# Layer 1's first norm on places that are free early and with its roots in PSUM; layer 1's second modulation range computed beside layer 0's latent attention; half of layer 0's last scatter in place

## The chip, the cores and the metric

The kernel runs on one NeuronCore of a Trainium2 chip. Its engines run side by side, each through its own instruction queue in order: TensorE (PE in the profile; PEld is its weight loading), VectorE (DVE), ScalarE (ACT), GpSimd (POOL) and SyncE (SP), whose queue issues nearly all DMAs. The metric is the device time of one execution in microseconds; three runs of the kernel before gave a median of 1532.29 us (1531.54 to 1534.32).

## The reference

A backbone of two layers over 256 latent and 256 context tokens of 1024 channels, in float32. Each layer is a mixer and then a mixture of experts (MoE); both are entered through an RMS norm with a scale and shift ("modulation") computed from a condition vector, and left through a gate.

```
ml = split(silu(c) @ ada_w[l] + ada_b[l], 6)      # six modulation vectors; mc likewise from c_ctx
n  = rmsnorm(h, norm1_g[l]) * (1 + ml[1]) + ml[0]
h  = h + ml[2] * mixer(n)                          # layer 0: conv + differential attention; layer 1: gated linear attention
n  = rmsnorm(h, norm2_g[l]) * (1 + ml[4]) + ml[3]
h  = h + ml[5] * hier_moe(n)                       # 32 experts, top group of 4, top 2 of 8 inside it
rmsnorm(x, g) = x / sqrt(mean(x^2) + eps) * g
```

Layer 0 computes all 512 tokens; layer 1 ends with the 256 latent ones. The output is the latent stream.

## The kernel before

The program is written straight through as mixer0, the MoE of layer 0, mixer1, the MoE of layer 1. The tile framework gives every engine its queue by its own estimate of times and by priorities (a stretch written under `later()` is put behind), so a line that is moved can change the order of others around it. `order` rows below show the queues that came out.

*Tokens.* `H` holds the residual stream, four blocks of 128 tokens (blocks 0 and 1 latent, 2 and 3 context). `XH` and `XL` hold the mixer's or MoE's transposed input, split into a rounded part and a rest, so that a product is three TensorE passes (`mm3`, L288 to L293).

*Weights.* `wtile()` hands out 1 MB places of a ring, four in the mixers and more in the MoEs. A load into a place waits until the place's earlier weights have been read. A weight is split by `quarter` (L366 to L373): ACT rounds it (`wh`, L371), POOL or DVE subtracts (`wl`, L372).

*Modulation.* `ada_steps(l, r, ...)` computes range r (0, 1 or 2, a third of the six vectors each) in eight steps. A step loads 1 MB of `ada_w` (L196) and does four matmuls of 32 x 512 (L201); the eighth adds the bias (L210). It is a generator: each `next()` is one step, so the steps can be laid among other work. `ada_cols` (L267, L270) transposes range 0 into columns that the norm uses.

*mixer0.* After the projections come four attention blocks (`attn_block`), two latent and two context. Each block's four heads call `fill(i)`; for the latent blocks `fill_lat` takes one step of `ada_steps(1, 0)`, for the context blocks `fill_ctx` takes two quarters of the latent rows' output projection (`out_lat`). The four loads of `ab_w_out` (`ts`, L359) use the same ring of four as the `ada` steps and stand behind them on SP.

*MoE of layer 0.* `scatter0` (L1491 to L1502) adds a pair of expert groups to `H`: for each of four blocks and two halves of the channels four matmuls into one of two `wk` PSUM banks (L1498), a multiplication by the gate into an SBUF tile `sc` (L1501, DVE), and an addition to `H` (L1502: POOL for half 0, DVE for half 1). The last call ends the MoE and feeds mixer1.

*mixer1.* `norm_mod_T` (L318 to L342), called for the latent and then the context stream, squares two blocks on ACT (L325) into tiles `xn` of the pool `raw1`, takes the reciprocal roots on DVE (`rstd_of`, L273 to L286: nine instructions on 128x2, all in SBUF), scales (L328 on DVE, L329 on ACT), transposes on PE (L335), modulates on DVE (L340), rounds on ACT to `XH` (L341) and subtracts to `XL` (L342: DVE for even k, POOL for odd). The small weights of the decay (`wf`, L820 to L827) are loaded by SP and split by ACT (L874, L879) and DVE (L875, L880). `ada_steps(1, 1)` runs here, its eight loads into four tiles that are free then (`S`, `sg`, `bT`, `attb`). The q projection follows (L870), then k, decay, levels, v, gate and output.

Of the kernel before, what the change touches and what calls it, by code (L numbers as in the profile page):

```python
# [9 lines left out]
FT = mybir.dt.float32  # L10
FR = mybir.dt.float32r
BF = mybir.dt.bfloat16
I32 = mybir.dt.int32
U32 = mybir.dt.uint32
AF = mybir.ActivationFunctionType
OP = mybir.AluOpType
# [3 lines left out]
D = 1024  # L20
# [10 lines left out]
EPS = 1e-6  # L31
# [49 lines left out]
def trunk_kernel(ctx: ExitStack, tc: tile.TileContext, A: dict, out: bass.AP):  # L81
    nc = tc.nc
# [9 lines left out]
    def pj(dt=FT):  # L92
        return psum.tile([128, 512], dt, name="pj", tag="pj", bufs=4)
# [6 lines left out]
    def wk(dt=FT):  # L100
        return wkp[0].tile([128, 512], dt, name="wk", tag="wk", bufs=2)
# [39 lines left out]
    H = const.tile([128, 4, D], FT, name="H")  # L141
# [112 lines left out]
    cols1 = [None]  # L254
# [18 lines left out]
    def rstd_of(dst, ss, n, pool, temps=None):  # L273
# [9 lines left out]
        for a in (2.38924456, 3 / c ** 2):  # L283
            nc.vector.tensor_mul(t, dst, dst)
            nc.vector.tensor_mul(t, t, w)
            nc.vector.scalar_tensor_tensor(dst, t, -a, dst, op0=OP.add, op1=OP.mult)  # L286

    def mm3(ps, st, mv, k0, k1):  # L288

        (sh, sl), (mh, ml) = st, mv  # L290
        nc.tensor.matmul(ps, sh, mh, start=k0, stop=False)  # L291
        nc.tensor.matmul(ps, sh, ml, start=False, stop=False)  # L292
        nc.tensor.matmul(ps, sl, mh, start=False, stop=k1)  # L293
# [21 lines left out]
                else:  # L315
                    nc.scalar.activation(o, v, AF.Copy)

    def norm_mod_T(pool, st, cols):  # L318

        ss = pool.tile([128, 2], FT, name="ss", tag="ss", bufs=2)  # L320
        rs = pool.tile([128, 2], FT, name="rs", tag="rs", bufs=2)
        xs = []
        for i in range(2):
            x = pool.tile([128, D], FT, name="xn", tag="xn", bufs=4)
            nc.scalar.activation(x, H[:, 2 * st + i], AF.Square, accum_out=ss[:, i:i + 1])  # L325
            xs.append(x)
        rstd_of(rs, ss, D, pool)
        nc.vector.tensor_scalar(xs[0], H[:, 2 * st], rs[:, 0:1], None, op0=OP.mult)  # L328
        nc.scalar.activation(xs[1], H[:, 2 * st + 1], AF.Copy, scale=rs[:, 1:2])  # L329
        t = slice(256 * st, 256 * st + 256)  # L330
        for kp in range(4):
            ps = trps()
            for j in range(4):
                k = 2 * kp + j // 2
                nc.tensor.transpose(ps[:, j * 128:(j + 1) * 128], xs[j % 2][:, k * 128:(k + 1) * 128], ident)  # L335
            for kk in range(2):
                k = 2 * kp + kk
                v = ps[:, kk * 256:kk * 256 + 256]
                a = pool.tile([128, 256], FT, name="xa", tag="xa", bufs=4)
                nc.vector.tensor_scalar(a, v, cols[:, 1, k, st:st + 1], cols[:, 0, k, st:st + 1], op0=OP.mult, op1=OP.add)  # L340
                nc.scalar.activation(XH[:, k, t], a, AF.Copy)  # L341
                (nc.gpsimd if kk else nc.vector).tensor_sub(XL[:, k, t], a, XH[:, k, t].bitcast(FT))  # L342
# [56 lines left out]
    def mixer0():  # L399
        es = ExitStack()  # L400
        with es:
# [3 lines left out]
            bp = pool(es2, "b0", "left")  # L405
# [310 lines left out]
                    k = 2 * q + kk  # L716
                    mm3(ps, (ch[:, k, t], cl[:, k, t]), (w[0][:, kk], w[1][:, kk]), k == 0, k == 7)

            ad = ada_steps(1, 0, bp)
            ts = []  # L720

            def fill_lat(i):
                next(ad, None)

            def out_lat():
                for n in range(2):
# [19 lines left out]
                attn_block(b, fill_lat)  # L746
            for _ in ad:
                pass
            cols1[0] = ada_cols(1)
            ts += [load_cols(w, [(512 * n, 512)]) for n in range(2)]  # L750
            es6.close()
            es2.close()
# [31 lines left out]
    def mixer1():  # L784
        es = ExitStack()
        with es:
# [44 lines left out]
            def split2(x0, x1):  # L831

                hl = [xp.tile([128, 1024], FR, name="w" + t, tag="ws" + t, bufs=3) for t in "hl"]
                for i, x in enumerate((x0, x1)):
# [8 lines left out]
            tsq = load_cols(w_in, [(0, 512)])  # L843


            free = [S.rearrange("p a h e -> p (a h e)"), sg.rearrange("p b c -> p (b c)"),
                    bT.rearrange("p a h t -> p (a h t)"), attb]

            fill = ada_steps(1, 1, mp, free[::-1])
            cols = cols1[0]  # L850
            for st in range(2):
                norm_mod_T(rp, st, cols)
            for _ in fill:
                pass
            es2.close()
            es4 = ExitStack()
            lp = pool(es4, "gl1", "right")
# [14 lines left out]


            nc.scalar.activation(wa2s[0], wa2, AF.Copy)  # L874
            nc.vector.tensor_sub(wa2s[1], wa2, wa2s[0].bitcast(FT))  # L875
            wah, wal = (ep.tile([128, 8, 128], FR, name="wv", tag="Ev", bufs=3) for _ in range(2))
            w4 = [waf.rearrange("p k (d j) -> p k d j", d=2)] + [w.rearrange("p k (d c j) -> p k d c j", d=2, c=2) for w in (wah, wal)]
            for c in range(2):
                nc.scalar.activation(w4[1][:, :, :, c], w4[0], AF.Copy)  # L879
                nc.vector.tensor_sub(w4[2][:, :, :, c], w4[0], w4[1][:, :, :, c].bitcast(FT))  # L880
            ps = wk()
            for k in range(8):
                mm3(ps, (wah[:, k], wal[:, k]), (xh[:, k], xl[:, k]), k == 0, k == 7)
# [352 lines left out]
    def moe(M):  # L1236
# [15 lines left out]
        with es:  # L1252
# [99 lines left out]
            with es2:  # L1352
# [135 lines left out]
                            if last:  # L1488
                                (nc.scalar if hf else nc.sync).dma_start(out[0, b * 128:(b + 1) * 128, c], H[:, b, c])

                def scatter0(Gs, ys):  # L1491

                    for b in range(nb):
                        for hf in range(2):
                            ps = wk()
                            n = 2 * len(Gs)
                            for i in range(n):
                                nc.tensor.matmul(ps, Gs[i // 2][:, b * 128:(b + 1) * 128], ys[i // 2][i % 2][:, hf], start=i == 0, stop=i == n - 1)  # L1498
                            c = slice(512 * hf, 512 * hf + 512)
                            t = ep.tile([128, 512], FT, name="sc", tag="sc", bufs=2)  # L1500
                            nc.vector.tensor_mul(t, ps, g2[:, b // 2, c])  # L1501
                            (nc.vector if hf else nc.gpsimd).tensor_add(H[:, b, c], H[:, b, c], t)  # L1502
# [233 lines left out]
                if l == 0:  # L1736
# [24 lines left out]
                    for j in range(0, NG, 2):  # L1761
# [29 lines left out]
                        prev = ([G[:, x] for x in range(2)], ys)  # L1791
                        if nxt:
                            (xgT, G), gc = nxt, gcn
                    scatter0(*prev)
                else:
                    P0 = group_hot(groups[0], pos0)
                    crowded()
# [57 lines left out]
```

## Time and profile before

| what | value |
|---|---|
| median of three runs | 1532.29 us |
| profiled execution | 1534.05 us, of which the trace's span 1532.3 us |
| PE busy | 1287.3 us (84% of the span) |
| DVE, ACT, POOL busy | 573.5, 367.9, 280.0 us |
| DMA | 498.10 MB, mean 325 GB/s |

The profile covers one execution. Its page gives the busy time of each engine, 40 slices of the span, the DMA queues, the chain of work that ended last, and the costliest groups of instructions. The trace behind it can be asked for the instructions of a stretch in order of time, or for the busy time of each engine in given stretches. The granted clock of TensorE (PEclk) is a share of full speed: 1.00 is 2.4 GHz and 0.50 is 1.2 GHz. The stages of the kernel by the trace: mixer0 to about 340 us, the MoE of layer 0 to about 835, mixer1 to about 1060, the MoE of layer 1 to the end.

### The profile page before, as it was taken

What the parts mean: (1) busy time and instruction counts of PE and PEld (TensorE: products, weight loads), DVE (VectorE), ACT (ScalarE), POOL (GpSimd) and SP (SyncE); (2) the same over time, 40 slices, a digit from 0 to 9 for tenths busy, and PEclk for the clock granted to TensorE, in tenths of its full rate; (3) what the DMA queues carried; (4) which work ended last, traced back from release to release, by engine and by line L of the source; (5) the groups of instructions that cost most, each with busy time, mean ns of one, the idle gap of its engine ahead of it and who ended that gap; (6) DMA issues with size and microseconds to landing.
All of it is one profiled execution on the core that took longest, in us unless ns stands there. A gap on an engine that the chain in (4) does not pass through costs nothing. (4 is left out here: it accounts for less than half of the span.)

```text
span 1532.3 us, 19009 instructions
## 1 busy us (share of the span) xinstructions
PE 1287.3 (84%) x7485; PEld 659.9 (43%) x7485; DVE 573.5 (37%) x1182; ACT 367.9 (24%) x700; POOL 280.0 (18%) x190
## 2 busy tenths in 40 slices
PE   5998978788789899999987999997966778777776
PEld 4665636564234344443422677775412222222221
DVE  4489895753002131221205546766202012112111
ACT  3245563441010101010102484434100000000000
POOL 1467601421001010100103543452000000000000
PEclk9999997798999999999998999999898889999889
DMA  9857361156999999999999634468799999999996
GB/s 318 286 203 248 118 220 51 64 203 280 421 422 424 422 422 422 376 423 422 423 423 390 221 101 138 166 224 323 299 426 427 426 427 427 427 427 427 427 427 281
DMA packets 101133, 498.10 MB, mean 325 GB/s; under 512 B 17654, under 2 KB 30297, under 8 KB 46253
## 3 DMA queue, kind: packets, MB, share of 16 engines
q1 hardware_dynamic: 96796, 489.84, 79.7%
q0 software_dynamic: 1680, 6.16, 1.3%
q8 instruction: 61, 1.00, 0.2%
q10 hardware_dynamic: 2560, 0.81, 0.2%
q14 instruction: 36, 0.29, 0.0%
HBM read 495.68 MB, written 1.10 MB: 324 GB/s over the span
## 5 line engine op out<-in xcount | busy, mean ns | idle before, releaser
L1561 PE MATMUL pj<-wx,xgT 128*32 128x512 f32 (+1 forms) x1496 | 312.8, 645 | 70.1 <-DMA wx<-in_moe_w_dram 70.1
L1561 PE MATMUL pj<-wt,xgT 128*32 128x512 f32 (+1 forms) x704 | 164.4, 639 | 26.4 <-DMA wt<-in_moe_w_dram 22.5
L1561 PEld LDWEIGHTS pj<-wx,xgT 128*32 128x32 f32 (+1 forms) x1496 | 75.7, 120 | 256.5 <-DMA wx<-in_moe_w_dram 130.6
L1570 PE MATMUL pj<-wx,hT 128*32 128x512 f32 (+1 forms) x792 | 166.7, 604 | 9.1 <-DMA wx<-in_moe_w_dram 5.1
L1453 DVE SCALAR_TENSOR_TENSOR s<-s,gc,pj 128x512 f32<-128x512 f32 x20 | 14.9, 747 | 421.6 <-PE pj L1561 368.3
L372 POOL TENSOR_TENSOR wl<-wt,wh 128x1024 fp32r<-128x1024 f32 x50 | 124.8, 2504 | 159.8 <-ACT wh L371 152.8
L291 PE MATMUL pj<-wh,XH 128*128 128x512 f32 x304 | 124.4, 419 | 17.2 <-ACT p L623 9.6
L292 PE MATMUL pj<-wl,XH 128*128 128x512 f32 x304 | 125.1, 411 | 1.6 <-POOL wl L372 1.5
L293 PE MATMUL pj<-wh,XL 128*128 128x512 f32 x304 | 123.7, 408 | 0.2
L1502 POOL TENSOR_TENSOR H<-H,sc 128x512 f32<-128x512 f32 x24 | 30.7, 1278 | 396.6 <-DVE sc L1501 396.6
L371 ACT ACTIVATE wh<-wt 128x1024 fp32r<-128x1024 f32 x66 | 68.9, 1055 | 66.7 <-PE pj L293 46.7
L1561 PEld LDWEIGHTS pj<-wt,xgT 128*32 128x32 f32 (+1 forms) x704 | 38.4, 120 | 104.9 <-issue 58.7
L1570 PEld LDWEIGHTS pj<-wx,hT 128*32 128x32 f32 (+1 forms) x792 | 42.6, 113 | 93.0 <-issue 70.5
L291 PEld LDWEIGHTS pj<-wh,XH 128*128 128x128 f32 x304 | 59.2, 196 | 46.7 <-ACT p L623 11.0
L1452 ACT ACTIVATE s<-pj 128x512 f32<-128x512 f32 x20 | 12.0, 598 | 252.7 <-PE pj L1561 252.7
L1458 ACT ACTIVATE hT<-trps 128x512 f32<-128x512 f32 x20 | 11.9, 597 | 247.3 <-PE trps L1456 247.3
L545 DVE SCALAR_TENSOR_TENSOR wk<-hp,vt,wk 128x512 f32<-128x512 f32 x90 | 67.5, 750 | 1.7
L292 PEld LDWEIGHTS pj<-wl,XH 128*128 128x128 f32 x304 | 59.7, 196 | 18.1 <-issue 3.2
L293 PEld LDWEIGHTS pj<-wh,XL 128*128 128x128 f32 x304 | 59.4, 195 | 14.5 <-DVE XL L1096 1.2
L1570 PE MATMUL pj<-wt,hT 128*32 128x512 f32 (+1 forms) x280 | 56.0, 611 | 2.8 <-ACT hT L1458 2.8
L1388 PE MATMUL wk<-P,XH 128*128 128x256 f32 x192 | 50.8, 300 | 5.2 <-ACT xgT L1390 3.8
L1501 DVE TENSOR_TENSOR sc<-wk,g 128x512 f32<-128x512 f32 x48 | 32.2, 687 | 44.2 <-PE wk L1498 44.2
(470 smaller groups left out, 1980.1 us busy)
## 6 DMA issues: line engine op xcount, KB each, us to landing
wx<-in_moe_w_dram SPq DMA_DIRECT2D x266, 1024.0 KB, 19.6
wt<-in_moe_w_dram SPq DMA_DIRECT2D x107, 1024.0 KB, 19.4
wa<-in_ada_w_dram SPq DMA_DIRECT2D x16, 1024.0 KB, 4.9
wt<-in_gla_w_in_dram SPq DMA_DIRECT2D x12, 1024.0 KB, 7.9
H<-in_moe_w_dram SPq DMA_DIRECT2D x11, 1024.0 KB
S<-in_ada_w_dram SPq DMA_DIRECT2D x10, 1024.0 KB, 12.9
wt<-in_ada_w_dram SPq DMA_DIRECT2D x8, 1024.0 KB, 6.9
wt<-in_ab_w_in_dram SPq DMA_DIRECT2D x6, 1024.0 KB, 11.6
```

What stands on the lines that cost most here:

```text
L291: nc.tensor.matmul(ps, sh, mh, start=k0, stop=False)
L292: nc.tensor.matmul(ps, sh, ml, start=False, stop=False)
L293: nc.tensor.matmul(ps, sl, mh, start=False, stop=k1)
L371: nc.scalar.activation(wh, w, AF.Copy)
L372: (nc.vector if dve or alt and q % 2 else nc.gpsimd).tensor_sub(wl, w, wh.bitcast(FT))
L545: e.scalar_tensor_tensor(av, hp[:, cb, :, t:t + 256], cw[:, t, cb:cb + 1], av, op0=OP.mult, op1=OP.add)
L1388: nc.tensor.matmul(ps[:, k], M['X'][h][:, k0 + k, b * 128:(b + 1) * 128], P[:, b], start=b == 0 and h == 0, stop=b == nb - 1 and h == 1)
L1453: nc.vector.scalar_tensor_tensor(s, s, gc, h3, op0=OP.mult, op1=OP.mult)
L1501: nc.vector.tensor_mul(t, ps, g2[:, b // 2, c])
L1502: (nc.vector if hf else nc.gpsimd).tensor_add(H[:, b, c], H[:, b, c], t)
L1561: nc.tensor.matmul(ps[o:o + w], xgT[:, k, o:o + w], W[nm, x, k // 4][:, k % 4], start=k == 0, stop=k == 7)
L1570: nc.tensor.matmul(ys[hf][o:o + w], hT[:, k, o:o + w], W["2", x, k // 2][:, k % 2, hf * 512:(hf + 1) * 512], start=k == 0, stop=k == 3)
```

## The change

Four edits.

1. `ada_steps(1, 1)` leaves mixer1. In mixer0 a generator `early` chains range 0, `ada_cols(1)` and range 1, and `fill_lat` takes two steps per head where it took one. Its loads now go through the ring of four.
2. `norm_mod_T` writes its squares and scaled rows into halves of `S` and `sg` in place of `xn` tiles, and calls a new `rstd_free`: the same root, with most of its values in a `wk` PSUM bank, so that every instruction has a PSUM operand. It takes eleven instructions in place of nine.
3. The three subtractions of the decay weights go from DVE to POOL.
4. In the last `scatter0` call, half 1 of each block is summed in a `pj` bank, multiplied there, and added to `H` from there by DVE.

```diff
+    def rstd_free(dst, ss, n, pool):
+        c = 0.703952253
+        k2 = (0.5 * c ** 3) ** 2
+        m = ss.shape[-1]
+        t = pool.tile(list(ss.shape), FT, name="rst", tag=f"rsq{m}t", bufs=2)
+        b = wk()
+        w, d0, d, t2 = (b[:, i * m:(i + 1) * m] for i in range(4))
+        nc.vector.tensor_scalar(w, ss, 1.0 / (n * k2), EPS / k2, op0=OP.mult, op1=OP.add)
+        nc.vector.tensor_scalar(d0.bitcast(I32), w.bitcast(I32), 1, None, op0=OP.logical_shift_right)
+        for o in (dst, d):
+            nc.vector.tensor_scalar(o.bitcast(I32), d0.bitcast(I32), -1.0, float(0x5F1FFFF9), op0=OP.mult, op1=OP.add)
+        for i, a in enumerate((2.38924456, 3 / c ** 2)):
+            nc.vector.tensor_mul(t, d, dst)
+            nc.vector.tensor_mul(t2, w, t)
+            if i == 0:
+                nc.vector.scalar_tensor_tensor(d, t2, -a, dst, op0=OP.add, op1=OP.mult)
+            nc.vector.scalar_tensor_tensor(dst, t2, -a, dst, op0=OP.add, op1=OP.mult)
...
-    def norm_mod_T(pool, st, cols):
+    def norm_mod_T(pool, st, cols, xs):
...
-            x = pool.tile([128, D], FT, name="xn", tag="xn", bufs=4)
-            nc.scalar.activation(x, H[:, 2 * st + i], AF.Square, accum_out=ss[:, i:i + 1])
-            xs.append(x)
-        rstd_of(rs, ss, D, pool)
+            nc.scalar.activation(xs[i], H[:, 2 * st + i], AF.Square, accum_out=ss[:, i:i + 1])
+        rstd_free(rs, ss, D, pool)
...
-            ad = ada_steps(1, 0, bp)
+            def early():
+                yield from ada_steps(1, 0, bp)
+                cols1[0] = ada_cols(1)
+                yield from ada_steps(1, 1, bp)
+            ad = early()
...
-                next(ad, None)
+                for _ in range(2):
+                    next(ad, None)
...
-            cols1[0] = ada_cols(1)
...
-            free = [S.rearrange("p a h e -> p (a h e)"), sg.rearrange("p b c -> p (b c)"),
-                    bT.rearrange("p a h t -> p (a h t)"), attb]
-            fill = ada_steps(1, 1, mp, free[::-1])
+            free = [S.rearrange("p a h e -> p (a h e)"), sg.rearrange("p b c -> p (b c)")]
...
-                norm_mod_T(rp, st, cols)
-            for _ in fill:
-                pass
+                norm_mod_T(rp, st, cols, [free[st][:, i * D:(i + 1) * D] for i in range(2)])
...
-            nc.vector.tensor_sub(wa2s[1], wa2, wa2s[0].bitcast(FT))
+            nc.gpsimd.tensor_sub(wa2s[1], wa2, wa2s[0].bitcast(FT))
...
-                nc.vector.tensor_sub(w4[2][:, :, :, c], w4[0], w4[1][:, :, :, c].bitcast(FT))
+                nc.gpsimd.tensor_sub(w4[2][:, :, :, c], w4[0], w4[1][:, :, :, c].bitcast(FT))
...
-                            ps = wk()
+                            ps = pj() if last and hf else wk()
...
+                            if last and hf:
+                                nc.vector.tensor_mul(ps, ps, g2[:, b // 2, c])
+                                nc.vector.tensor_add(H[:, b, c], H[:, b, c], ps)
+                                continue
...
-                    scatter0(*prev)
+                    scatter0(*prev, last=True)
```

The queues that come out. First PE in mixer0's latent attention, from the end of the first eight modulation steps (L201) on; L614 (new L630) are the score products, L291 and its neighbours the output projection. Before:

```order
L201 MATMUL wk<-wt,st_81 32x512 x4
L614 MATMUL pj<-kT,qT 128x512 x4
L614 MATMUL pj<-kT,qT 128x256 x4
L291 MATMUL pj<-wh,XH 128x512
L292 MATMUL pj<-wl,XH 128x512
```

And of the changed kernel (L656 and L650 are the old L640 and L634, L685 the old L669):

```order
L201 MATMUL wk<-wt,st_81 32x512 x4
L630 MATMUL pj<-kT,qT 128x512 x2
L201 MATMUL wk<-wt,st_81 32x512 x4
L630 MATMUL pj<-kT,qT 128x512 x2
L201 MATMUL wk<-wt,st_81 32x512 x4
L630 MATMUL pj<-kT,qT 128x256 x2
L201 MATMUL wk<-wt,st_81 32x512 x4
L630 MATMUL pj<-kT,qT 128x256 x2
L201 MATMUL wk<-wt,st_81 32x512 x4
L685 MATMUL trps<-cst,o_1934 128x128 x4
L650 MATMUL trps<-cst,p 128x128 x4
L656 MATMUL wk<-V,at 128x128 x4
```

Four of the new steps stand between the score products; the other four stand among the next products of the block, and the output projection begins behind the last of them.

Second, ACT at the start of mixer1: squares, rounded weights (`wh`), scaled rows, decay weights (`wv`, `wa2h`) and rounded inputs (`XH`). Before:

```order
L325 ACTIVATE xn,ss<-H 128x1024 x4
L371 ACTIVATE wh<-wt 128x1024 x3
L329 ACTIVATE xn<-H,rs 128x1024 x2
L341 ACTIVATE XH<-xa 128x256 x7
L879 ACTIVATE wv<-wf 128x16x32 x2
L874 ACTIVATE wa2h<-wf 128x512
L341 ACTIVATE XH<-xa 128x256
```

Of the changed kernel:

```order
L342 ACTIVATE S,ss<-H 128x1024 x2
L342 ACTIVATE sg_6105,ss<-H 128x1024 x2
L387 ACTIVATE wh<-wt 128x1024 x3
L345 ACTIVATE S<-H,rs 128x1024
L896 ACTIVATE wv<-wf 128x16x32 x2
L345 ACTIVATE sg_6105<-H,rs 128x1024
L891 ACTIVATE wa2h<-wf 128x512
L357 ACTIVATE XH<-xa 128x256 x10
```

The decay weights were behind seven of the `XH` instructions and are now ahead of all of them.

Third, POOL in the same place (the `wf` tile is cleared, then loaded by SP). Before:

```order
L820 MEMSET wf 128x1024
L812 CAST tri<-qk 128x512
L814 COPY lv<-qk 128x192
L815 COPY b_6056<-qk 128x1
L372 TENSOR_TENSOR wl<-wt,wh 128x1024 x3
L342 TENSOR_TENSOR XL<-xa,XH 128x256 x4
```

Of the changed kernel:

```order
L833 CAST tri<-qk 128x512
L835 COPY lv<-qk 128x192
L836 COPY b_6108<-qk 128x1
L841 MEMSET wf 128x1024
L388 TENSOR_TENSOR wl<-wt,wh 128x1024 x3
L897 TENSOR_TENSOR wv<-wf,wv 128x16x32 x2
L892 TENSOR_TENSOR wa2l<-wf,wa2h 128x512
L358 TENSOR_TENSOR XL<-xa,XH 128x256 x5
```

The clearing of `wf` went behind three copies, and the three decay subtractions came in ahead of the first `XL`.

## Rows read from the trace of the kernel before

**Rows 1.** The page's part 4, the chain that ended last, by line.
```profile
DMA wx<-in_moe_w_dram 15%; DMA wt<-in_moe_w_dram 6%; PE pj L1570 1%; PE pj L1561 1%; PE wk L1408 0%; PE wk L1484 0%; DVE pj L1466 0%; ACT XH L1468 0%; DVEq L1851 0%; DVE s L1453 0%; PE trps L1456 0%; DVE H L1487 0%; ACT hT L1458 0%; PE pj L1484 0%; PE trps L1417 0%
```
**Rows 2.** Busy us per stretch: PE, PEld, DVE, ACT, POOL, clock, DMA share, GB/s.
```profile
355.00:366.00 11.00, 11.00 (x89) 7.00 (x91) 2.37 (x8) 1.79 (x3) 0.00 (x0) 1.00 0.02 6
...
1067.00:1090.00 23.00, 15.24 (x91) 7.46 (x95) 9.66 (x50) 3.32 (x6) 0.00 (x0) 0.70 0.38 135
```
**Rows 3.** DVE in order of time (start, us, line, operation) around mixer1's start.
```profile
825.00 1.37 DVE L1501 TENSOR_TENSOR sc<-wk,g 128x512 f32<-128x512 f32 x2
...
833.87 1.26 DVE L1502 TENSOR_TENSOR H<-H,sc 128x512 f32<-128x512 f32 x1
...
837.16 0.16 DVE L285 TENSOR_TENSOR rst<-rst,rsw 128x2 f32<-128x2 f32 x1
...
838.42 2.24 DVE L282 TENSOR_SCALAR rs<-rs 128x2 int32<-128x2 int32 x1
...
843.00 2.28 DVE L285 TENSOR_TENSOR rst<-rst,rsw 128x2 f32<-128x2 f32 x1
...
846.77 1.44 DVE L340 TENSOR_SCALAR xa<-trps,cols 128x256 f32<-128x256 f32 x3
```
**Rows 4.** DVE, the same multiplication done in place at mixer1's end.
```profile
1049.67 1.29 DVE L1109 TENSOR_TENSOR pj<-pj,g 128x512 f32<-128x512 f32 x2
```
**Rows 5.** ACT at mixer1's start; in brackets the idle time before.
```profile
832.98 1.06 ACT L325 ACTIVATE xn<-H 128x1024 f32<-128x1024 f32 x1 [8.62 <-PE wk L1498]
...
847.34 0.87 ACT L341 ACTIVATE XH<-xa 128x256 fp32r<-128x256 f32 x2
```
**Rows 6.** POOL at mixer1's start.
```profile
838.27 6.99 POOL L372 TENSOR_TENSOR wl<-wt,wh 128x1024 fp32r<-128x1024 f32 x3 [1.82 <-ACT wh L371]
```
**Rows 7.** SP's queue, DMA issues at mixer1's start (start, us of the issue).
```profile
825.44 0.84 SPq L196 DMA_DIRECT2D S<-in_ada_w_dram  x1
...
835.50 7.93 SPq L823 DMA_DIRECT2D wf<-in_gla_w_in_dram  x2
843.49 3.43 SPq L826 DMA_DIRECT2D wf<-in_gla_w_a_dram  x1
...
849.35 0.27 SPq L827 DMA_DIRECT2D wf<-in_gla_b_a_dram  x1
```
**Rows 8.** The decay weights' issues: us from issue to landing.
```profile
DMA to landing us min/median/max: 1.7/1.7/1.8
```
**Rows 9.** PE from the q projection's first product to the k projection's.
```profile
848.28 0.48 PE L870 MATMUL pj<-XH,wh 128*128 128x256 f32 x2
...
881.60 0.39 PE L291 MATMUL pj<-wh,XH 128*128 128x512 f32 x1
```
**Rows 10.** The stretch between, L201's instructions alone: PE and PEld busy, clock, DMA.
```profile
848.20:881.60 33.40, 7.24 (x40) 0.96 (x40) 0.95 0.68 247
```
**Rows 11.** L201 alone, mixer0's eight steps.
```profile
202.00:217.40 15.40, 7.69 (x64) 1.67 (x64) 1.00 0.86 341
```
**Rows 12.** Stretches of mixer0's attention, columns as in rows 2.
```profile
217.40:232.10 14.70, 7.90 (x16) 3.50 (x16) 14.00 (x38) 8.91 (x18) 0.00 (x0) 0.75 0.72 216
232.10:250.00 17.90, 17.52 (x94) 14.57 (x94) 7.18 (x12) 7.24 (x14) 1.61 (x2) 0.92 0.00 1
250.00:261.60 11.60, 8.10 (x25) 5.23 (x24) 8.59 (x35) 4.89 (x17) 2.08 (x4) 0.74 0.06 11
```
**Rows 13.** SP there: the issues of the output weights.
```profile
212.02 5.79 SPq L359 DMA_DIRECT2D wt<-in_ab_w_out_dram  x4
```
**Rows 14.** PE there: the output projection's first product.
```profile
232.14 0.80 PE L291 MATMUL pj<-wh,XH 128*128 128x512 f32 x1 [0.22 <-ACT p L623]
```
**Rows 15.** DVE there: one of the three weight subtractions of 222 to 227 us.
```profile
222.26 1.22 DVE L372 TENSOR_TENSOR wl<-wt,wh 128x1024 fp32r<-128x1024 f32 x1
```
**Rows 16.** PE, groups of 217.40 to 261.60: busy, mean ns, idle before.
```profile
L614 PE MATMUL pj<-kT,qT 64*128 64x256 f32 (+1 forms) x32 | 14.3, 596 | 10.1 <-ACT p L623 10.1
...
L640 PE MATMUL wk<-V,at 128*128 128x128 f32 x32 | 4.1, 275 | 0.0
```

More of the change, by code (lines that the diff above doesn't have):

```diff
@@ L316, in norm_T @@
                     nc.scalar.activation(o, v, AF.Copy)
-    def norm_mod_T(pool, st, cols):
+    def norm_mod_T(pool, st, cols, xs):
         ss = pool.tile([128, 2], FT, name="ss", tag="ss", bufs=2)
         rs = pool.tile([128, 2], FT, name="rs", tag="rs", bufs=2)
-        xs = []
         for i in range(2):
-            x = pool.tile([128, D], FT, name="xn", tag="xn", bufs=4)
-            nc.scalar.activation(x, H[:, 2 * st + i], AF.Square, accum_out=ss[:, i:i + 1])
-            xs.append(x)
-        rstd_of(rs, ss, D, pool)
+            nc.scalar.activation(xs[i], H[:, 2 * st + i], AF.Square, accum_out=ss[:, i:i + 1])
+        rstd_free(rs, ss, D, pool)
         nc.vector.tensor_scalar(xs[0], H[:, 2 * st], rs[:, 0:1], None, op0=OP.mult)
@@ L1489, in scatter, with scatter0 @@
                                 (nc.scalar if hf else nc.sync).dma_start(out[0, b * 128:(b + 1) * 128, c], H[:, b, c])
-                def scatter0(Gs, ys):
+                def scatter0(Gs, ys, last=False):
                     for b in range(nb):
                         for hf in range(2):
-                            ps = wk()
+                            ps = pj() if last and hf else wk()
                             n = 2 * len(Gs)
```

## The prediction

> **What bounds the kernel now.** I read the page's chain first: it ends in weight loads of the last MoE, DMA alone holding 21% of the span in its first two groups [rows 1]. Then busy time by stretch at the entry of each MoE. There the weight stream stands still: DMA share 0.02 in 355 to 366 and 0.38 in 1067 to 1090, while PE is busy without a gap (11.00 of 11.0, 23.00 of 23.0) [rows 2]. The ring is full and waits until PE's first products of the MoE have read a place. From there each stream runs to the stage's end, and its bytes don't change. So what ends a mixer earlier or later moves the total by as much, and I work out two shifts: of mixer1's end and of mixer0's.
>
> At mixer1's start the reader is to see three chains that end almost together. DVE finishes the scatter at 833.87 + 1.26 = 835.13, and three root instructions of 128x2 take 2.24 to 2.28 us (the first at 838.42, the last at 843.00) where a neighbour takes 0.16 [rows 3]; through all of them POOL runs three subtractions, 6.99 us from 838.27 [rows 6]. ACT squares the last block from 832.98, after waiting 8.62 us for PE's last scatter product [rows 5]. SP needs from 835.50 to 849.62 to issue the four loads of the decay weights, behind 4 MB of modulation weights issued from 825.44 on [rows 7]. PE starts the q projection at 848.28 and the k projection at 881.60 [rows 9]; within that, the modulation products take 7.24 us (40 of them: five of the eight steps) [rows 10].
>
> **Mixer1, part by part.** *Scatter.* Before, twelve DVE instructions fill 825.00 to 835.13 [rows 3]: eight multiplications and four additions slowed beside POOL. Four halves now have an operand in PSUM. The nearest row, the same multiplication in place, takes 1.29/2 = 0.65 us [rows 4], so 12 x 0.64 = 7.7 us: the end moves to about 832.7, 2.4 us earlier. Four SBUF-only multiplications may stay slow, so the gain lies between 0 and 2.4.
>
> *Squares.* They no longer wait for a tile that PE's scatter must free (the 8.62 us), and follow each block. The last one moves with the scatter: about 835.3.
>
> *Roots.* The first three slow instructions lose 3 x (2.26 - 0.16) = 6.3 us if an instruction with a PSUM operand doesn't wait for POOL; two more per stream cost 4 x 0.2 = 0.8. With the scatter's 2.4 the first modulation (L340, 846.77 [rows 3]) would come at 846.77 - 6.3 + 0.8 - 2.4 = 838.9. Two kinds stay with SBUF operands alone, the scaling (old L328) and the rest (old L342), so up to 3.7 us may come back (one and a half of the slow row's 2.3): 842.6.
> The Trainium skill, page "SBUF — State Buffer", section "Who interferes with whom", says that a VectorE instruction with two SBUF inputs contends with a GpSimd instruction that reads SBUF, the one that comes second being blocked for the other's whole length, and that one with at most one SBUF input outside the 2-port modes does not. The 0.16 against 2.28 agrees for two inputs. By the same rule the edit that puts three more subtractions on POOL is a price and no relief: they lengthen the stretch in which old L342 on DVE can be blocked, which is inside the 842.6 above.
>
> *The decay weights.* This is where I see the new limit. In the rows of order ACT's `wv` and `wa2h` now stand ahead of every `XH`, so PE's q projection waits for the landing of `wf`. The modulation loads are gone from SP's queue. Last landing: at best four issues like that of 825.44, 835.8 + 4 x 0.84 + 1.7 = 840.9 [rows 7, 8]; at worst what it was, 849.35 + 0.27 + 1.7 = 851.3. I take all four issues as long as the first row alone, 7.93: 835.8 + 7.9 + 1.7 = 845.4, near the middle. After it `wa2h` takes about 0.5 us (half of the 1.06 of an instruction twice its size) and from XH to PE it is 848.28 - 847.34 = 0.94 [rows 5, 9]: the q projection starts at 846.8. At best (840.9 for the landing, DVE between 838.9 and 842.6) it is about 843, at worst 852.8.
>
> *Products.* From its start to the k projection PE took 33.3 us, of which 7.24 was modulation, spaced 6.9: 26.4 are left. 846.8 + 26.4 + 1.5 = 874.7, the 1.5 being my allowance for the rests `XL`, which POOL makes only after six subtractions of weights. Against 881.60 that is **-7**. Best 843 + 26.4 = 869.4, -12.2; worst 852.8 + 26.4 + 1.5 = 880.7, -0.9.
>
> **Mixer0.** Eight steps cost PE 7.69 us as in the first range [rows 11]. The cover is the idle time of the latent attention: 14.7 - 7.90 = 6.8, then 0.4, then 11.6 - 8.10 = 3.5, 10.7 in all [rows 12], of which 10.1 stand ahead of the score products, waiting for the softmax on ACT [rows 16]. By the order the first four steps lie between those score products; they take 3.85 us of the 6.8 and cost nothing, provided their weights are there: the output weights in their place were issued from 212.02 on [rows 13], and 1 MB takes 3.1 us at the 341 GB/s of rows 11. The softmax itself hangs on DVE, 14.00 of 14.7 busy; the three weight subtractions of 1.22 us each [rows 15] leave this stretch, since those weights come later: 3.66 us earlier for the first block's end.
>
> The other four steps and the output projection are the price. The projection began at 232.14 [rows 14]. Its weights now come behind steps 13 to 16, read until about 236, plus 3.1 for the first MB and some 2 for its rounding and subtraction: 240 to 243. In between stand the four steps (3.85) and products that the softmax releases earlier (value products, 4.1 us [rows 16], and the transposes before them). The work put off goes beside the second block's scores, where 3.5 us were idle. So 3.85 - 3.5 = +0.35 if the softmax's advance is lost, -3.3 if it is kept; I take the middle, **-1.5**. Bounds: if all idle time were used, 7.7 - 10.7 - 3.7 = -6.7, and with the clock at 1.00 in place of 0.75 for 7.90 us another -2.0, -8.7; if the projection starts at 243 and nothing comes earlier, +10.9. Later stretches I take to keep their length.
>
> **Sum.** The profiled execution took 1534.05 us (1532.3 of span, 1.75 around it). -7 - 1.5 = -8.5 gives 1525.5 for it, and as it lies 1.76 above the median of the runs, **1523.8** for the median.
>
> **Rivals.**
> *More.* The attention also uses its idle time (-5 to -8.7): 1532.3 - 7 - 7 = 1518, with the start at 843 down to 1512. For it: 10.1 us of PE's idle time has one cause, and it moves earlier. Against: the late output weights.
> *No change.* `wf` lands at about 851 although the modulation loads are gone, because its own many small pieces make the time: -0.9 in mixer1 and +0.35 in mixer0, 1531.8. For it: the second `wf` issue took 3.43 us [rows 7] when most of the modulation weights had landed. Against: at 827 to 843 the queue had 4 MB ahead, and 247 GB/s ran through the whole stretch [rows 10].
> The Trainium skill, page "DMA: Bandwidth & Descriptors", section "Why small descriptors are slow (HBM only)", says that each piece carries a fixed cost, which speaks for this rival; no row here shows these loads on an empty queue.
> *Slower.* The output projection can't begin before 243, and as the second block's scores come no earlier, the work put off isn't recovered: +10.9 - 7 = +3.9, 1536.2. It decides from a start of about 242.2, where +10.1 is 3.1 more than mixer1's -7. For it: the loads of a ring of four wait for four more readers; PE was busy 17.52 of 17.9 us in the stretch that is emptied [rows 12]. Against: the 3.66 us of DVE.
>
> **Chances.** Forecast (1518.5 to 1529) 0.50; more 0.19; no change 0.15; slower 0.16. A measurement of this kernel tells about 0.2% (3 us) from no change, so faster is the first two, 0.69, same 0.15, slower 0.16. Of the slower case half lies above 1536 and of "more" a fifth or so below 1513, so the range 1513 to 1536 leaves out some 0.12 plus what I haven't thought of; the forecast's own range is 1518.5 to 1529.
>
> **What will show it.** Right: root instructions at 0.2 to 0.3 us beside POOL; the last scatter addition near 832.7 by old times; the last `wf` landing 10 us after its first issue; the q projection some 14 us after the last scatter addition, with ACT's first `XH` released by `wa2h`; 28 us from there to the k projection; four steps between the first score products without an idle wait for DMA; the second block's scores near 246. Wrong: tiny DVE instructions of 2 us left in the norm's root (mixer1 gains 3 at most); an idle PE ahead of the first output product, beyond 242; PE waiting on `XL` for more than 2 us; or a MoE whose stream isn't set back by its mixer's end, in which case no shift passes on.

## The result, and the profile after

The changed kernel took 1520.81 us (median of four, 1520.18 to 1522.43), before 1531.91 (four runs): ratio 0.9925, 95% interval 0.9913 to 0.9938, 11.1 us less. 1523.8 was predicted. The profiled execution took 1520.93, span 1519.2; the profiled one of before lies 2.1 above its median, so its 13.1 us of difference hold some chance.

I cut each span at five events: the router's first count products after mixer0 (M0: `trps<-Aa` of PE, old L1316; the expectations call them the router transposes), the end of the last scatter addition on DVE, the first q product, the first k product, and the router's first count products after mixer1 (M1). Each column is the time since the one before. The experiments stand beside, as the sections below use them; all are single profiled executions, the last column is the median of the runs.

| kernel | M0 | to scatter's end | to q | to k | to M1 | to the end | median |
|---|---|---|---|---|---|---|---|
| before | 347.50 | 487.63 | 13.15 | 33.32 | 188.39 | 462.3 | 1531.91 |
| changed | 341.20 | 484.59 | 10.21 | 30.25 | 190.43 | 462.5 | 1520.81 |
| e1: edit 1 alone | 343.80 | 485.75 | 14.76 | 24.83 | 185.56 | 464.2 | 1520.34 |
| e2: thin steps | 341.43 | 482.63 | 9.61 | 30.17 | 190.16 | 459.9 | 1519.42 |
| e3: without edit 3 | 341.85 | 485.02 | 11.17 | 27.21 | 185.53 | 459.8 | 1513.32 |
| e4: decay weights held | 343.75 | 484.80 | 9.31 | 25.21 | 190.82 | 464.4 | 1519.68 |
| e5: edits 1 and 2 | 341.42 | 487.39 | 10.27 | 28.04 | 188.71 | 464.0 | 1516.88 |
| e6: as e3, roots in SBUF | 343.74 | 484.84 | 15.49 | 26.20 | 185.57 | 460.1 | 1519.72 |
| e7: before, output weights on POOL | 339.67 | 486.12 | 14.19 | 31.87 | 187.38 | 463.7 | 1526.75 |
| e8: as e3, decay weights held | 341.42 | 484.82 | 9.31 | 27.28 | 190.88 | 462.4 | 1518.11 |
| e9: changed again | 343.75 | 484.83 | 10.22 | 30.26 | 190.48 | 462.3 | 1521.24 |
| e10: e3 again | 345.24 | 485.05 | 11.17 | 27.31 | 187.76 | 463.3 | 1519.68 |
| e11: as e3, output weights on POOL | 351.69 | 484.54 | 11.18 | 27.10 | 187.81 | 464.1 | 1524.60 |
| e12: as e3, every second one on POOL | 337.91 | 484.57 | 10.92 | 26.67 | 185.75 | 463.5 | 1511.77 |

Mixer0 ends 6.3 us earlier, the scatter brings 3.0, mixer1 from there 4.0, and the last MoE keeps its length. So the shifts pass on, as argued from [rows 2]. The column "to scatter's end" holds more than the scatter: the scatter's twelve DVE instructions begin 475.1 to 477.5 us after M0 in these profiles, and from their first to their end take 7.5 us in all kernels with edit 4, 10.1 in the four without (before, e1, e5, e7).

The latent attention after, the stretches of [rows 12] (PE, PEld, DVE, ACT, POOL, clock, DMA share, GB/s):

```profile
217.40:232.10 14.70, 11.16 (x64) 4.61 (x65) 12.56 (x40) 7.91 (x19) 0.00 (x0) 1.00 1.01 366
232.10:250.00 17.90, 15.29 (x94) 9.55 (x93) 10.98 (x37) 9.82 (x23) 1.11 (x2) 0.90 0.99 351
250.00:261.60 11.60, 11.60 (x51) 8.56 (x50) 6.97 (x12) 3.86 (x4) 5.88 (x8) 1.00 0.73 196
```

PE does 4.5 us more in all and the granted clock of the first stretch is 1.00 where it was 0.75. The second block's scores of before, then PE's scores and waits of after:

```profile
250.25 2.22 PE L614 MATMUL pj<-kT,qT 64*128 64x256 f32 x8 [0.24 <-ACT p L623]
```

```profile
240.91 1.13 PE L630 MATMUL pj<-kT,qT 64*128 64x256 f32 x4 [0.78 <-ACT p L639]
...
297.32 0.79 PE L310 MATMUL pj<-wh,XH 128*128 128x512 f32 x1 [12.54 <-ACT p L639]
```

And the same last wait of before, for the softmax of the last block:

```profile
300.94 0.80 PE L291 MATMUL pj<-wh,XH 128*128 128x512 f32 x1 [9.35 <-ACT p L623]
```

PE reaches that wait 6.8 us earlier (284.8 against 291.6), waits 3.2 longer, and needs 2.7 less for the 118 instructions behind it (20.9 against 23.6). In the wait it is DVE that works: 9.18 of 9.4 us before, 12.06 of 12.5 after. In its queue the modulation of the MoE's input (L1228) and its rests (L1232) stand ahead of the last softmax's scaled maxima (L618). Before:

```profile
291.18 2.48 DVE L1228 SCALAR_TENSOR_TENSOR x<-x,rs,B 128x1024 f32<-128x1024 f32 x2
...
297.52 2.00 DVE L1232 TENSOR_TENSOR XL<-x,XH 128x1024 fp32r<-128x1024 f32 x1
299.42 0.17 DVE L618 SCALAR_TENSOR_TENSOR nb<-mx,sq 128x4 f32<-128x4 f32 x1
```

mixer1's start, on DVE (to [rows 3]):

```profile
825.11 0.68 DVE L1519 TENSOR_TENSOR H<-H,pj 128x512 f32<-128x512 f32 x1
825.71 0.15 DVE L296 TENSOR_SCALAR wk<-ss 128x2 f32<-128x2 f32 x1
...
830.99 0.16 DVE L305 SCALAR_TENSOR_TENSOR rs<-wk,rs 128x2 f32<-128x2 f32 x1
...
835.52 1.70 DVE L358 TENSOR_TENSOR XL<-xa,XH 128x256 fp32r<-128x256 f32 x1 [0.41 <-ACT XH L357]
```

No root instruction exceeds 0.17; the SBUF-only `L358` still takes 1.70 beside POOL. SP's issues of the decay weights (to [rows 7]), the time from issue to landing of those at `L844` and at `L847` (to [rows 8]), and ACT, which works without a gap of more than 0.12 us from 828.24 to the first `XH`:

```profile
829.04 1.01 SPq L844 DMA_DIRECT2D wf<-in_gla_w_in_dram  x2
830.10 0.66 SPq L847 DMA_DIRECT2D wf<-in_gla_w_a_dram  x1
...
832.85 0.27 SPq L848 DMA_DIRECT2D wf<-in_gla_b_a_dram  x1
```
```profile
DMA to landing us min/median/max: 2.3/2.3/2.3
```
```profile
DMA to landing us min/median/max: 1.8/1.8/1.8
```
```profile
828.24 2.93 ACT L387 ACTIVATE wh<-wt 128x1024 fp32r<-128x1024 f32 x3
831.08 1.13 ACT L345 ACTIVATE S<-H,rs 128x1024 f32<-128x1024 f32 x1
832.24 1.15 ACT L896 ACTIVATE wv<-wf 128x512 fp32r<-128x512 f32 x2
833.30 1.13 ACT L345 ACTIVATE sg<-H,rs 128x1024 f32<-128x1024 f32 x1
834.55 0.63 ACT L891 ACTIVATE wa2h<-wf 128x512 fp32r<-128x512 f32 x1
835.09 1.32 ACT L357 ACTIVATE XH<-xa 128x256 fp32r<-128x256 f32 x4
```

POOL (to [rows 6]) and PE (to [rows 9]):

```profile
829.42 7.52 POOL L388 TENSOR_TENSOR wl<-wt,wh 128x1024 fp32r<-128x1024 f32 x3 [0.41 <-POOL wf L841]
836.89 2.88 POOL L897 TENSOR_TENSOR wv<-wf,wv 128x512 fp32r<-128x512 f32 x2
839.74 1.44 POOL L892 TENSOR_TENSOR wa2l<-wf,wa2h 128x512 fp32r<-128x512 f32 x1
841.14 3.83 POOL L358 TENSOR_TENSOR XL<-xa,XH 128x256 fp32r<-128x256 f32 x5
```
```profile
836.00 0.73 PE L887 MATMUL pj<-XH,wh 128*128 128x256 f32 x2
...
842.87 1.08 PE L351 MATMUL trps<-cst,sg 128*128 128x128 f32 x4 [2.86 <-DVE xa L356]
...
866.25 0.39 PE L310 MATMUL pj<-wh,XH 128*128 128x512 f32 x1
```

The q projection starts early and then waits: POOL's first rest `XL` comes at 841.14, behind 4.3 us of decay subtractions, and PE runs without a gap only from 842.87. PE's wait of 2.86 us is for DVE's `xa`; by the code `xa` has four buffers, and POOL's rests have to free them, so that this wait hangs on POOL too. That link is read from the code; e3 below bears it out.

### The profile page after: what moved, and what is told of

It is laid out like the page before. It is cut to its first block, busy times and chain, and to the rows that moved or that the text cites. A ratio compares the mean times of both kernels' runs of the same rounds, so it can differ in the third digit from the quotient of the medians.

```text
span 1519.2 us, 19024 instructions
## 1 busy us (share of the span) xinstructions
PE 1279.6 (84%) x7485; PEld 656.5 (43%) x7485; DVE 566.4 (37%) x1183; ACT 367.4 (24%) x700; POOL 283.7 (19%) x193
## 5 line engine op out<-in xcount | busy, mean ns | idle before, releaser
L1582 PE MATMUL pj<-wt,xgT 128*32 128x512 f32 (+1 forms) x704 | 154.4, 622 | 23.7 <-DMA wt<-in_moe_w_dram 21.4
L310 PE MATMUL pj<-wh,XH 128*128 128x512 f32 x304 | 121.5, 412 | 19.9 <-ACT p L639 12.5
L1405 PE MATMUL wk<-P,XL 128*128 128x256 f32 x192 | 49.8, 294 | 0.0
```

The costliest lines, as they stand in the source:

```text
L1405: nc.tensor.matmul(ps[:, k], M['X'][h][:, k0 + k, b * 128:(b + 1) * 128], P[:, b], start=b == 0 and h == 0, stop=b == nb - 1 and h == 1)
L1582: nc.tensor.matmul(ps[o:o + w], xgT[:, k, o:o + w], W[nm, x, k // 4][:, k % 4], start=k == 0, stop=k == 7)
```

## The experiments

**e1, edit 1 alone**, on the kernel before:

```diff
-            ad = ada_steps(1, 0, bp)
...
+            ad = early()
...
-                next(ad, None)
+                for _ in range(2):
+                    next(ad, None)
...
-            fill = ada_steps(1, 1, mp, free[::-1])
...
```

> The kernel before with edit 1 alone (the second modulation range beside the latent attention); norm, roots, decay subtractions and scatter as before. Theory A (the changed kernel's gain of 11 us is about half mixer0's, half mixer1's, and in mixer1 the freed start of the norm is worth its own part): mixer0's last router transposes at 341 as in the changed kernel, where before had them at 347.5; mixer1 loses the modulation products, but the roots blocked beside POOL and the squares that wait for the scatter stay, so the total is 3 to 6 us above the changed kernel, 1524 to 1527. Theory B (only the products that PE no longer does in mixer1 and the attention count, the norm's start being hidden): the changed kernel's time within 2 us, 1519 to 1523.

Measured 1520.34 (1518.45 to 1520.63): theory B's time. Edits 2 to 4 together bring nothing that shows. By stages the changed kernel gains 4.6 us up to the q projection (10.21 against 14.76) and 1.2 at the scatter, then loses 5.4 to the k projection and 4.9 to M1: 4.6 lost in all from M0 to M1. The totals are alike only because e1's profile has mixer0 2.6 and the last MoE 1.7 longer, both with code that is the same in the two kernels and both at a lower granted clock (shown below). B's reason, that the norm's start is hidden, is thus borne out in part: of what edits 2 to 4 together bring ahead of the q projection nothing is left at M1. Edit 1 alone takes 9.7 us out of the stretch from the scatter's end to M1 (234.86 to 225.15), most of it between q and k (33.32 to 24.83).

**e2, the moved steps thinned.**

```diff
-            nc.tensor.matmul(ps[32 * g:32 * g + 32], st32[:, k], w[:, g * 512:(g + 1) * 512], ...)
+            nc.tensor.matmul(ps[32 * g:32 * g + 32, :n], st32[:, k], w[:, g * 512:g * 512 + n], ...)
```

Here `n` is 32 in range 1 of layer 1 and 512 elsewhere.

> The changed kernel with the eight moved steps reduced on PE: each still loads its 1 MB and reads it with four products, but of 32 columns instead of 512, so PE has some 7 us less to do in the latent attention, and the modulation is left incomplete. Theory A (the steps fill gaps in which PE would wait for the softmax, and the granted clock, 0.76 before and 1.00 after in 217 to 232, stays up through them): without the filling the clock falls to 0.75 to 0.85 again, score and output products take as long as before, and mixer0's router transposes come at 344 to 347 instead of 341.2: total 3 to 6 us above the changed kernel although PE has less to do. Theory B (the gain is the order: the weight subtractions gone from DVE and the output projection behind the second block's scores): transposes at 336 to 341, total 0 to 5 us below the changed kernel.

1519.42 (1515.70 to 1520.94), M0 341.43. A's clock came and A's time did not:

```profile
217.40:232.10 14.70, 10.90 (x67) 5.89 (x66) 13.70 (x41) 7.77 (x18) 0.00 (x0) 0.81 1.02 370
```

PE is busy for 10.90 us at 0.81 with a sixteenth of the steps' columns, for 11.16 at 1.00 with all. The steps' products cost no time there, since the clock gives it back; but they are not what brings M0 forward. What is left is the late output weights and the orders that come with them, on PE and on DVE.

**e3, edit 3 undone.**

```diff
-            nc.gpsimd.tensor_sub(wa2s[1], wa2, wa2s[0].bitcast(FT))
+            nc.vector.tensor_sub(wa2s[1], wa2, wa2s[0].bitcast(FT))
...
-                nc.gpsimd.tensor_sub(w4[2][:, :, :, c], ...)
+                nc.vector.tensor_sub(w4[2][:, :, :, c], ...)
```

> The changed kernel with edit 3 undone: the three decay subtractions on DVE again, between the first modulated tiles. Theory A (POOL is the limit at the start of the q projection: its first rest XL comes at 841.1 behind 4.3 us of decay subtractions, and PE's products run without a gap only from 843.6): XL on POOL at about 837, PE without a gap from 839.5 to 840.5, total 2 to 4 us below the changed kernel. Theory B (a subtraction with two SBUF operands on DVE waits for POOL's three of 2.5 us): the modulated tiles come 3 to 6 us later, PE without a gap from 845 on, total 1 to 4 us above it.

1513.32 (1512.36 to 1514.31), lower than A's 2 to 4 us. Both mechanisms are there: POOL's first `XL` comes at 838.42 (11.6 after the scatter's end; 15.4 in the changed kernel), and the first decay subtraction on DVE took 2.16 for B's reason. The q projection starts 1.0 later than in the changed kernel and the k projection comes 3.0 sooner behind it, so that A wins by 2.1. The rest lies later. In the changed kernel PE stops for the levels, and DVE's instruction that it waits for runs into a POOL subtraction:

```profile
912.48 2.04 PE L1007 MATMUL wk<-Ev 128*128 128x128 f32 x8 [3.53 <-DVE Ev L1029]
```
```profile
908.97 3.36 DVE L1029 TENSOR_TENSOR Ev<-Ev,qk 128x1024 f32<-128x1024 f32 x1
```
```profile
908.83 5.72 POOL L388 TENSOR_TENSOR wl<-wt,wh 128x1024 fp32r<-128x1024 f32 x2 [3.28 <-ACT wh L387]
```

In e3 PE's queue has those products behind 21 more projection products, and they find their input ready; two such DVE instructions take 2.35 together:

```profile
906.73 2.35 DVE L1029 TENSOR_TENSOR Ev<-Ev,qk 128x1024 f32<-128x1024 f32 x2
```

**e4, the decay weights held back** (subtractions on POOL):

```diff
+            for o in (wa2s[0][:, 0:32], wah[:, 0, 0:32]):
+                nc.scalar.activation(o, XH[:, 7, 0:32].bitcast(FT), AF.Copy)
```

> The changed kernel with the decay weights' rounding on ACT and their subtractions on POOL held back until the eight latent XH are made (by two 32-column copies that read the last of them). Theory A (as for the kernel with the subtractions on DVE: POOL's 4.3 us ahead of the rests are the limit): the first XH 1 us earlier, XL on POOL at 837, PE without a gap from about 839.5, total 3 to 5 us below the changed kernel. Theory B (PE only does other things in another order; the decay products, the levels and what follows come later by as much): within 1 us of it.

1519.68 (1512.91 to 1522.95). The start is A's: to q 9.31, to k 25.21, 5.9 us better than the changed kernel in the two together. The wait for the levels stays (190.82 to M1), and in this profile M0 and the last stage are 2.5 and 1.9 longer with the same code in them. So the median can't decide; the stages bear out A for the start alone.

**e5, edits 1 and 2.** As e3, and

```diff
-                    scatter0(*prev, last=True)
+                    scatter0(*prev)
```

> Edits 1 and 2 alone (modulation moved; squares, rows and roots of the norm as in the changed kernel), with the last scatter and the decay subtractions as before. The kernel with edits 1, 2 and 4 took 1513.3. Theory A (the norm starts when the last block of the scatter is in H, so the scatter's 2.4 us pass on): 2 to 3.5 us above it, 1515.3 to 1516.8, with the last addition of the scatter about 2.5 us later after mixer0's end. Theory B (the scatter's end is hidden behind POOL's additions and subtractions): within 1 us of 1513.3.

1516.88 (1514.85 to 1521.53). The scatter's end comes 487.39 after M0 against 485.02: 2.4 us, as A and the prediction have it; the twelve DVE instructions alone take 2.6 us more (10.12 against 7.51). The totals overlap with those of e3 and e10, so the time alone doesn't show it.

**e6, roots in SBUF.** As e3, and

```diff
-        rstd_free(rs, ss, D, pool)
+        rstd_of(rs, ss, D, pool)
```

> Edits 1, 2 and 4 with the root in its old form, nine instructions in SBUF; all else as in the kernel that took 1513.3. Theory A (root instructions with two SBUF operands wait for POOL's subtractions, and the modulated tiles stand behind them on DVE): three to five root instructions of 2 to 2.5 us, the first modulated tile 5 to 9 us later, total 1518 to 1522. Theory B (with the squares now earlier, the roots run before POOL's subtractions begin, or the wait is hidden behind the rests that POOL owes): within 1.5 us of 1513.3.

1519.72 (1517.32 to 1522.40). DVE beside POOL's three subtractions:

```profile
832.28 2.83 DVE L344 TENSOR_SCALAR S<-H,rs 128x1024 f32<-128x1024 f32 x1 [0.42 <-DVE rsw L280]
835.04 2.32 DVE L281 TENSOR_SCALAR rs<-rsw 128x2 int32<-128x2 int32 x1
837.39 2.26 DVE L282 TENSOR_SCALAR rs<-rs 128x2 int32<-128x2 int32 x1
839.69 0.16 DVE L284 TENSOR_TENSOR rst<-rs 128x2 f32<-128x2 f32 x1
```
```profile
832.21 7.42 POOL L388 TENSOR_TENSOR wl<-wt,wh 128x1024 fp32r<-128x1024 f32 x3 [0.40 <-POOL wf L841]
```

The two root instructions end at 837.36 and 839.65, with POOL's second and third subtraction; the next, after POOL's last, takes 0.16. The first modulated tile and the q projection are late by 4.3 us (15.49 against 11.17), but 1.0 of it comes back by the k projection. That is A's mechanism, with two slow root instructions and 4.3 us where A had three to five and 5 to 9. The total lies in A's range but shows nothing: e10, with the new roots, took 1519.68.

**e7, before with the output weights' subtractions on POOL.**

```diff
-                    w = quarter(xp, ts[n], q, 3, dve=True)
+                    w = quarter(xp, ts[n], q, 3)
```

> The kernel before with one thing changed: the subtractions of the eight quarters of the output weights go from DVE to POOL, which stands idle in 217 to 232. No modulation step is moved. Theory A (what brings mixer0's end forward is that DVE is relieved of the subtractions ahead of the softmax): the second block's score products come at 246 to 248 instead of 250.25, mixer0's router transposes at 343 to 345.5 instead of 347.5, total 2 to 4.5 us below before, 1528 to 1530.5. Theory B (what matters is that the output projection stands behind the second block's scores, since its weights come late): transposes at 346.5 to 349, total within 1.5 us of before.

1526.75 (1525.06 to 1530.76), M0 339.67: more than A's gain, and not where A has it. The second block's scores come where they came before:

```profile
250.74 2.22 PE L614 MATMUL pj<-kT,qT 64*128 64x256 f32 x8 [0.24 <-ACT p L623]
...
286.40 0.63 PE L669 MATMUL trps<-cst,o 128*128 128x128 f32 x4 [1.23 <-DVE o L666]
```
```profile
286.17 0.68 DVE L617 TENSOR_REDUCE mx<-pj 128x2 f32<-128x512 f32 x1
...
300.55 2.48 DVE L1228 SCALAR_TENSOR_TENSOR x<-x,rs,B 128x1024 f32<-128x1024 f32 x2
```

The wait of 9.35 us for the last softmax is gone: PE's queue has the last scores at 277.4 and 281.5 with 12 and 10 output products behind each, where before has them at 288.47 behind nearly all products that were ready. DVE's queue has the last softmax's maxima at 286.17, ahead of the MoE's input (L1228), where before has that input first. Both theories fall. One line of code on which engine subtracts moves mixer0 by 7.8 us between two single profiles. The orders of both queues change, and DVE is rid of the subtractions as well; which of these carries the gain is not isolated.

**e8, e3 with the decay weights held** behind the fourth `XH` (the two copies of e4, reading `XH[:, 3]`).

> Edits 1, 2 and 4, the decay subtractions on DVE, and the decay weights' rounding held behind the first four XH (by two 32-column copies on ACT that read the fourth). Theory A (in the kernel with 1513.3 the first two decay subtractions on DVE wait 2 us each for POOL ahead of the modulated tiles, so that the first XH is late by 3 us): first XH at about 11 us after the scatter's end, PE without a gap 1 to 2 us sooner, 1510.5 to 1512.5. Theory B (POOL's rests XL, behind its three weight subtractions, hold PE anyway): within 1 us of 1513.3.

1518.11 (1517.90 to 1519.01): neither. The q projection starts 1.9 us earlier as in A, the k projection gains 1.8 in all, and the levels' wait takes it back: 4.94 us ahead of their products at 912.98, 190.88 to M1.

**e9 and e10, the changed kernel and e3 once more**, unedited.

> The changed kernel once more, beside the kernel without edit 3 on one chip. Theory A (edit 3 is a loss of some 7 us): 1520 to 1522, and 6 to 9 us above the next. Theory B (the difference seen was one of chips and of the clock's chances): the two within 3 us of each other.

> The changed kernel without edit 3 once more. Theory A: 1512 to 1515. Theory B: 1516 to 1521, within 3 us of the changed kernel.

1521.24 and 1519.68: within 3 us, theory B's times. Over both sets of runs the changed kernel has nine runs from 1519.37 to 1523.72 (median 1520.9), e3 ten from 1512.36 to 1521.53 (median 1516.9). The stages that edit 3 touches repeat better: scatter's end to M1 is 230.9 and 231.0 with it, 223.9 and 226.2 without. So edit 3 costs 4.7 to 7.0 us there, but 1513.3 was a lucky set, not the kernel's level.

**e11 and e12, e3 with all, or every second, of the output weights' subtractions on POOL** (the line of e7; in e12 with `alt=True`).

> The kernel without edit 3, and the subtractions of the eight quarters of the output weights on POOL, as in the kernel that had this alone on top of before and gained 6 us. Theory A (that gain came from the order behind 262, where DVE has less to do ahead of the last softmax, and adds to the moved steps): mixer0's router transposes at 338 to 340.5 (341.2 to 343.8 with the steps moved alone), total 1508.5 to 1512. Theory B (both take the same wait, 9 to 12 us of PE ahead of the last softmax, and POOL's subtractions take twice DVE's time): transposes at 341 to 345, total 1513 to 1517.

> As the last, with every second quarter's subtraction on POOL and the others on DVE. Theory A: between the two, 1510 to 1513. Theory B: 1513 to 1516.

e11: 1524.60 (1522.30 to 1528.95), M0 351.69, worse than B has it. The two DVE instructions ahead of the router's bias products (PE L1196) run beside POOL's work and take 7.42 us, 0.81 before, and PE waits for them:

```profile
270.88 7.42 DVE L1188 TENSOR_TENSOR Ws<-Wr,AT 128x288 f32<-128x288 f32 x2 [1.39 <-DMA Wr<-in_re_w_dram]
```
```profile
278.43 1.07 PE L1196 MATMUL trps<-cst,bc__2216 36*128 36x36 f32 x4 [6.69 <-DVE bc__2216 L1193]
```

e12: 1511.77 (1506.78 to 1517.17), M0 337.91, the earliest of all: PE's longest wait up to 320 us is 4.27 us, ahead of scores, in place of 12.54:

```profile
249.95 3.17 PE L630 MATMUL pj<-kT,qT 64*128 64x256 f32 x8 [4.27 <-ACT p L639]
```

Here too DVE has the last softmax's maxima (289.05) ahead of the MoE's input (293.57).

e12 beats both kernels: 0.9866 of before (0.9846 to 0.9886), the changed kernel in the same set 0.9926 (0.9913 to 0.9938).

## Why the prediction was right, and where it wasn't

The median came out 3.0 us below the forecast and inside its range. In part that is luck: in the profiles mixer1's -7 came true as -9.1 up to the k projection and 2.0 lost behind it, two terms were mis-sized, and the wait that I called the new limit was not there.

- *Mixer0, -1.5: mis-sized.* It measured -6.3 in the profiles. The nine profiles with this mixer0 (changed, e1, e3 to e6, e8 to e10) give -6.3 to -2.3 against the one of before, median -3.8. The bound -8.7 held. The step that failed is "the work put off goes beside the second block's scores, where 3.5 us were idle". The second block's scores themselves came 9.3 us earlier, 240.91 against 250.25, since the products that stood ahead of them now stand behind. I looked at the idle time up to 261.6 and not at the 9.35 us of waiting for the last softmax, behind which PE works at the lower clock (0.50 in 301 to 306); PE now reaches it 6.8 us earlier. In e7 and e12 that wait is gone and mixer0 ends earliest, so the order that leads to it matters; whether PE's order or DVE's decides is not shown.
- *The slower rival's start came, its premise did not.* The first output product came at 244.02, later than its 242.2, but the second block's scores came earlier, and nothing was lost.
- *The steps' cost, nothing: right*, and for part of the reason given: their 3.85 us in the first stretch lie in its idle time, and the clock stayed at 1.00, where e2 with thin steps shows 0.81.
- *Scatter, 2.4: right.* The twelve instructions take 7.5 us where 7.7 were worked out; before they took 10.1. The "four SBUF-only multiplications" of the prediction do not exist, since every multiplication reads a `wk` bank: the slow rows of before were the four additions (1.20 to 1.29), which take 0.64 to 0.68 with a PSUM operand.
- *Roots, 6.3 less 0.8: right.* All at 0.15 to 0.17. e6 puts the way back to the old form at 4.3 us of the q projection's start.
- *The decay weights' landing, 845.4: wrong, and so is "PE's q projection waits for the landing of `wf`".* The first two issues took 1.01 us instead of 7.93, and `wa2h`, which needs the last landing, ran at 834.55, by before's axis 840.9 (6.3 later). That this is the best case to the tenth is luck: ACT has work without a gap from 828.24 to the first `XH`, so no wait for the landing shows, and it is ACT's own queue that sets the start. (The "four loads" are ten issues: two of `w_in`, four each of `w_a` and `b_a`.) The no-change rival, with the small pieces as its cause, is refuted: the first issues took 1.01 and 0.66 us where they took 7.93 and 3.43, and the loads landed 1.8 to 2.3 us after their issue. The 7.93 went away with the modulation weights ahead of them. The Trainium skill's section "Why small descriptors are slow (HBM only)" in "DMA: Bandwidth & Descriptors" was weighed for that rival; whatever that cost is for these loads, the trace shows no wait by it.
- *The allowance of 1.5 for the rests `XL`: mis-sized.* It measured 30.25 - 26.4 = 3.9 us, and its sign, "PE waiting on `XL` for more than 2 us", came in the 2.86 us ahead of 842.87. 3.0 of it go without edit 3 (27.21 in e3): I had counted POOL's six subtractions and then covered them. With an earlier start and a dearer wait the k projection came 9.1 us earlier by mixer0's end (-7 predicted, the two scatter and norm gains in it).
- *Behind the k projection nothing was to change; 2.0 us were lost* by the levels' wait (190.43 against 188.39). In e1, e3 and e6, where PE's order differs, that stage takes 185.5 to 185.6.
- *What the edits earn by M1.* From the scatter's first DVE instruction to M1 before takes 245.0 us, e1 235.3, e3 231.4, e10 233.8, the changed kernel 238.4 and e9 238.5. So edit 1 brings nearly all of mixer1's gain, edits 2 and 4 add 1.5 to 3.9, and edit 3 loses 4.6 to 7.1. The gains of roots and scatter are real where they arise, but most of them end in later waits.
- *Slips in the working.* 835.8 stands where the row has 835.50, and 3.7 where one and a half of 2.3 is 3.45; neither moves the forecast by more than 0.3.

That mixer0's stage ends anywhere from 341.2 to 345.2 with one and the same code goes with the granted clock in it. The four profiles that end at 341.2 to 341.9 (changed, e3, e5, e8) show 1.00 from 140 to 240 us; e4, e6 and e9 (343.7 to 343.8) show 0.83 in 230 to 240; e1 (343.8) 0.85 in 250 to 260, where the first four have 0.98 to 1.00; e10 (345.2) 0.77 to 0.92 in 130 to 160. Why the clock fell in one execution and not in another stays open. Of before there is one profile, so that its own spread is not known.

## What to carry to other kernels

Moving work beside a wait can pay more by what it pushes out of the way in the queues than by the idle time it fills: look for the longest wait of the whole stage, ask which engine works during it (here DVE, not the one that waits) and what stands ahead in its queue, and count from there. A gain at the start of a chain has to be followed to the stage's end: here most of the roots' and the scatter's ended in later waits. Handing an instruction to another engine costs what is queued behind it there (POOL's rests, here 3 us), and can cost again later (the levels' wait). Where one line of placement reorders a planned queue, try two or three placements and compare stages, not medians of few runs.

## What the runs showed of the hardware

Beside POOL's subtractions of 2.4 to 2.5 us, a DVE instruction of 128x2 took 2.26 to 2.32 even with one SBUF operand (e6), and never over 0.17 with an operand in PSUM. The Trainium skill's page "SBUF — State Buffer", "Who interferes with whom", names a second form that can be blocked, an instruction in a 2-port mode, which `tensor_scalar` can enter; the prediction cited only that with two inputs. Whether these ran in such a mode no row shows.

One kernel's executions can differ by 9 us (e3 and e10: 1512.4 to 1521.5), and part of that goes with the granted clock. The same five microseconds of the last MoE's start, ten after M1, in e3 and in e4:

```profile
1060.78:1065.78 5.00, 4.79 (x40) 1.86 (x38) 1.91 (x6) 0.07 (x1) 0.00 (x0) 1.00 0.00 0
```
```profile
1063.89:1068.89 5.00, 5.00 (x28) 2.68 (x30) 2.00 (x6) 0.07 (x1) 0.00 (x0) 0.50 0.00 0
```

The code is the same, and so are PE's waits between M1 and there (3.74 and 0.83 us); once 2.4 GHz is granted and once 1.2 GHz, and the stage takes 459.8 or 464.4 us. All fourteen profiles fall in line by the clock of these five microseconds: 459.8 to 460.1 us at 1.00 (e2, e3, e6), 462.3 to 462.5 at 0.66 to 0.70 (before, changed, e8, e9), 463.3 to 464.4 at 0.50 (the other seven).
